# Retention values of two heads projected in one pass of 512 moving columns, after all kv blocks

## The chip, the core and the metric

One NeuronCore of a Trainium2 chip runs the whole program; seven others are idle. The metric is the device time of one execution in microseconds (us), as the median of several. TensorE (PE) multiplies, ScalarE (ACT) and VectorE (DVE) move results out of its accumulators (PSUM, eight banks of 128 x 512 float32) and do the arithmetic between, GpSimd (POOL) does a few small steps, and SyncE (SP) issues the loads. Each engine works through a queue of its own; semaphores hold an instruction until what it reads is there.

## What is computed

One decoder block on 512 tokens of 1024 features, in float32. Cut to the part that the change touches:

```python
h = rmsnorm(x, pre_mix_norm)
proj = h @ w_in                     # (512, 5888)
q_r, k_r, v_r, g_r, q_s, k_s, v_s, gate_r, gate_s = split(proj)
ret = retention_chunkwise(q_r, k_r, v_r)     # 4 heads: dk 128, dv 256, chunks of 128 tokens
ret = silu(g_r) * ret
swa = swa_gqa_sinks(q_s, k_s, v_s, sinks)    # 8 query heads, 2 key/value heads of 64
merged = sigmoid(gate_r) * (ret @ w_ret_out) + sigmoid(gate_s) * (swa @ w_swa_out)
x = x + rmsnorm(merged @ w_out, post_mix_norm)
x = x + rmsnorm(square(relu(rmsnorm(x, pre_mlp_norm) @ w_up)) @ w_down, post_mlp_norm)
```

The values v_r of the four retention heads are columns 1024 to 2047 of the projection, 256 a head; the keys and values of the windowed attention (kv) are 256 columns more.

## The kernel before

Every float32 operand is split into a high and a low part that TensorE takes in one pass each (`split`, L104: ACT casts the high part, DVE subtracts for the low one), and a product is three matmuls (`mm3`, L147): high by high, high by low, low by high. Operands of weights are cast by `parts` (L112), into tiles `whi` and `wlo` of which four of each exist; loads land in two tiles `raw` of 1 MB.

The tokens are four blocks of 128. `norm_tokens` (L274) squares and sums a block on ACT, takes the power on POOL, scales on DVE (two instructions), transposes eight times on TensorE and splits the result into `hT`, features by tokens. A block can be projected in two ways. `project_block` (L312, tile `pblk`) has weights standing still and all 512 tokens moving: 24 matmuls of 512 columns give 128 output columns, features by tokens. `project_token_block` (L299, tile `ptok`) has one block of tokens standing still and 256 columns of weights moving: 24 matmuls of 256 columns give 128 tokens of 256 outputs. The values and the kv columns are wanted with tokens in rows, so they go the second way.

At the start (L338 to L350) the kv blocks and the value blocks of head 0 alternate: norm of token block 0, its kv block, norm of block 1, value block 0, kv block 1, norm of block 2, value block 1, and so on. Value block 3 follows later (L582), behind the first query projection and the transposes of the windowed keys. Then the loop over four heads (L583): scores of the windowed attention, projection of the retention queries, the output transposes of the head before, projection of the retention keys, transposes of the probabilities and keys, values of the *next* head (`project_v`, L305, in rounds 0 to 2), scores, windowed values, states, gates and, between the two gate blocks, the next head's windowed queries, and the retention outputs. The fourth round projects no values.

The order of the instructions in each engine's queue is settled when the program is built, from the order of the code, what each instruction depends on and which buffers are free, and is fixed from then on. The stretch around the change reads:

```python
    norm_tokens(0)
    w_kv = moving_parts(raw_kv)
    kv_block(0)
    norm_tokens(1)
    w_v0 = moving_parts(raw_v0)
    v0_block(0)
    kv_block(1)
```

Of the kernel before, what the change touches and what calls it, by code (L numbers as in the profile page):

```python
# [16 lines left out]
P = 128  # L17
D_MODEL = 1024
SEQ = 512
NT = SEQ // P  # L20
# [26 lines left out]
def decay_table():  # L47
    """[j, h, i]: gamma_h ** -(j + 1) / sqrt(dk) where i >= j, else 0; within a chunk."""
    pos = np.arange(P)
    t = np.where(  # L50
        pos[None, :] >= pos[:, None],
        np.exp(-log_gammas()[:, None, None] * (pos[:, None] + 1)), 0.0,
    )
    return np.ascontiguousarray((t * RET_DK**-0.5).transpose(1, 0, 2).astype(np.float32))


def chunk_table():
    """[j, 0, h]: gamma_h ** (127 - j) / sqrt(dk); [i, 1, h]: EPS * gamma_h ** (-2 (i + 1))."""
    pos, lg = np.arange(P)[:, None], log_gammas()[None, :]
    t = np.stack([np.exp(lg * (P - 1 - pos)) * RET_DK**-0.5, EPS * np.exp(-2 * lg * (pos + 1))], 1)  # L60
    return np.ascontiguousarray(t.astype(np.float32))


def distance_table():
    """[i, j]: distance of query i to key j of the two blocks, or MASKED / slope-free mask."""
    dist = (np.arange(P)[:, None] + P) - np.arange(2 * P)[None, :]
    return np.where((dist >= 0) & (dist < P), -dist, MASKED).astype(np.float32)
# [7 lines left out]
def block_kernel(ctx, tc, x, pre_mix, w_in, w_ret, w_swa, w_out, sinks, post_mix,  # L75
# [20 lines left out]
    def rstd_of(sumsq, n, scale):  # L96
        """(sumsq * scale + eps) ** -0.5, [P, n]."""
        ms = small.tile([P, 4], F32, name="ms")
        r = small.tile([P, 4], F32, name="rstd")
        nc.vector.tensor_scalar(ms[:, :n], sumsq, scale, EPS, op0=ALU.mult, op1=ALU.add)  # L100
        nc.gpsimd.tensor_tensor(r[:, :n], ms[:, :n], mhalf[:, :n], op=ALU.pow)
        return r

    def split(hi, lo, src):  # L104
        """src = hi + lo exactly, each with a significand that one pass carries."""
        nc.scalar.copy(hi, src)  # L106
        nc.vector.tensor_tensor(lo, src, f(hi), op=ALU.subtract)  # L107
# [10 lines left out]
    def load_feature_pair(w, c0):  # L118
        """Columns c0..c0+256 of w as two stationary blocks [k, kk, 128]."""
        nk = w.shape[0] // P  # L120
        raw = raw_tile([P, nk, 256])
        nc.sync.dma_start(raw, w[:, c0 : c0 + 256].rearrange("(k p) c -> p k c", p=P))
        return [parts(raw[:, :, b * P : (b + 1) * P], [P, nk, P]) for b in range(2)]

    def load_feature_blocks(w, cols):
        """Columns c..c+128 of w, for each c, as stationary blocks [k, kk, 128]."""
        nk = w.shape[0] // P
        raw = raw_tile([P, 2, nk, P])
        for b, c0 in enumerate(cols):
            nc.sync.dma_start(raw[:, b], w[:, c0 : c0 + P].rearrange("(k p) c -> p k c", p=P))  # L130
        return [parts(raw[:, b], [P, nk, P]) for b in range(len(cols))]

    def load_moving(w, r0, nr, c0, width):
        """Rows r0.. of w, columns c0..c0+width, as moving blocks, two tiles."""
        raw = raw_tile([P, nr, width])
        nc.sync.dma_start(
            raw, w[r0 * P : (r0 + nr) * P, c0 : c0 + width].rearrange("(k p) c -> p k c", p=P)
        )
        return moving_parts(raw)
# [12 lines left out]

    # ---- one level of Strassen-Winograd for a pair of output feature blocks:
    # rows of the product are the two blocks, its columns the two token halves,
    # the contraction is halved too.
    def wino_pool(stack, side="left"):
        return stack.enter_context(tc.tile_pool(name="wx", bufs=1, side=side))

    def wino_tokens(wx, b11, b12, b21, b22, f, dst):
        """b: (hi, lo) quadrants; f: their float32 copies, overwritten; dst: (hi, lo) of sums."""  # L160
        f11, f12, f21, f22 = f
        nc.vector.tensor_tensor(f11, f11, f12, op=ALU.subtract)
        split(dst[0][:, 0], dst[1][:, 0], f11)
        nc.vector.tensor_tensor(f12, f22, f12, op=ALU.subtract)
        split(dst[0][:, 2], dst[1][:, 2], f12)
        nc.vector.tensor_tensor(f22, f22, f11, op=ALU.add)
        split(dst[0][:, 1], dst[1][:, 1], f22)
        nc.vector.tensor_tensor(f21, f22, f21, op=ALU.subtract)
        split(dst[0][:, 3], dst[1][:, 3], f21)
        sums = [tuple(d[:, i] for d in dst) for i in range(4)]  # L170
        return {"11": b11, "21": b21, "22": b22, "t1": sums[0], "t2": sums[1],
                "t3": sums[2], "t4": sums[3]}

    def wino_weights(wx, w, c0):
        """Columns c0..c0+256 of w: the seven left operands, (hi, lo) of [k, 4, 128]."""
        raw = raw_tile([P, KD, 256])
# [22 lines left out]
    def wino_pair(wx, a, b, out):  # L199
        """out [P, 4, 256]: the two halves of block one, then those of block two, negated."""  # L200
        p16 = bank([P, 2, 256], "wino")
# [28 lines left out]

    # ---- pools by phase
    hctx = ExitStack()
# [3 lines left out]
    def transpose_in(dst, src_of, half):  # L236
        """token-major [P, 1024] blocks (of two token blocks) -> feature-major hi, lo."""
        for kp in range(KD // 2):
# [11 lines left out]

    # ---- pre-norm of x, kv and first v projection by token block
    bctx = ExitStack()
    kvpool = bctx.enter_context(tc.tile_pool(name="kvpool", bufs=1))
    kv = kvpool.tile([P, NT, 256], F32, name="kv")
    v_next = [kvpool.tile([P, NT, RET_DV], F32R, name=f"v{i}", bufs=2) for i in range(2)]
    xctx = ExitStack()
# [17 lines left out]
    def norm_tokens(t):  # L274
        """Token block t of the normed input, transposed, as hi and lo."""
        ss = small.tile([P, 2], F32, name="ss")
# [27 lines left out]

    def project_v(h):  # L305
        w = load_moving(w_in, 0, KD, C_VR + h * RET_DV, RET_DV)
        v = [kvpool.tile([P, NT, RET_DV], F32R, name=f"v{i}", bufs=2) for i in range(2)]
        for t in range(NT):
            split(v[0][:, t, :], v[1][:, t, :], project_token_block(w, t))
        return v  # L310

# [12 lines left out]
    load_x(1)  # L324
    raw_v0 = load_raw(C_VR)
    load_x(2)
# [5 lines left out]
    def kv_block(t):  # L332
        nc.scalar.copy(kv[:, t, :], project_token_block(w_kv, t))

    def v0_block(t):
        split(v_next[0][:, t, :], v_next[1][:, t, :], project_token_block(w_v0, t))

    norm_tokens(0)  # L338
    w_kv = moving_parts(raw_kv)
    kv_block(0)  # L340
    norm_tokens(1)
    w_v0 = moving_parts(raw_v0)
    v0_block(0)
    kv_block(1)
    norm_tokens(2)
    v0_block(1)
    kv_block(2)
    norm_tokens(3)
    v0_block(2)
    kv_block(3)  # L350
    xctx.close()
# [16 lines left out]

    # ---- sliding-window attention, one pair of heads (2b, 2b + 1)
    def swa_queries(w):  # L370
        """Both heads' scaled queries, each with hi and lo stacked along the contraction."""
        ps = project_block(w)
# [99 lines left out]

    # ---- retention, one head, by chunks of 128 tokens; token i of a chunk is carried
    # divided by gamma ** (i + 1), which the group norm takes out again
    def ret_keys(kT, h):
        """Token-major keys of the first three chunks, decayed to the chunk's end."""
        ps = bank([P, NT - 1, P], "ret_k")
# [23 lines left out]
    def ret_states(kd, v, h):  # L501
        """State before chunks 1, 2 and 3."""
        decayed = float(np.exp(log_gammas()[h] * P))
# [69 lines left out]
    for g in range(SWA_KV):  # L573
# [7 lines left out]
        split(ksT[0][:, g, :], ksT[1][:, g, :], ps)  # L581
    v0_block(3)  # L582
    for h in range(RET_HEADS):  # L583
# [13 lines left out]
        kd = ret_keys(kT, h)  # L597
        v = v_next
        if h + 1 < RET_HEADS:
            v_next = project_v(h + 1)  # L600
        pt = ret_scores(qT, kT, h)
# [14 lines left out]

    # ---- swa output projection
    def swa_out(fb, ws):
# [28 lines left out]

    # ---- gates
    gctx = ExitStack()
# [32 lines left out]
    def ret_proj(bp):  # L682
        """Output projection of the retention, gated, plus the gated swa's, in sig."""
        wr = load_feature_pair(w_ret, bp * 256)
# [18 lines left out]

    # ---- output projections of both mixers, merge
    mpool = ctx.enter_context(tc.tile_pool(name="mpool", bufs=16))
# [31 lines left out]

    # ---- output projection, residual, pre-norm of the MLP
    gpool = ctx.enter_context(tc.tile_pool(name="gpool", bufs=1, side="right"))
# [49 lines left out]

    # ---- MLP  # L790
    GB = 8
# [93 lines left out]
    def finish(t, n):  # L885
        """Post-norm and residual of token block t, once acc's column half n is whole."""
        c = slice(n * 512, (n + 1) * 512)
# [92 lines left out]
```

## Time and profile before

| | |
|---|---|
| median of 3 runs | 774.61 us (774.47 to 774.65) |
| span of the profiled execution, first to last instruction | 772.8 us |
| TensorE (PE) busy | 761.1 us |
| VectorE (DVE) busy | 510.3 us |
| ScalarE (ACT) busy | 367.6 us |
| mean granted TensorE clock | 0.997 of full speed |
| `ptok` matmuls, 256 columns | 480, of them 384 for values, 96 for kv |
| `pblk` matmuls, 512 columns | 480 |

The profiler records one execution. A line of the timeline gives the start in us, the duration, the engine, the line of the kernel, the operation, `output tile<-input tiles`, the shapes and how many instructions are merged in it; in brackets the idle time ahead of it and what ended it. Matmuls overlap in the record, so what one costs is the distance from start to start, not its duration. Lines of a helper such as L107 or L149 serve many callers; the tile names tell them apart.

### The profile page before, as it was taken

The page shows a single profiled execution, that of the slowest core. Times are in us where ns is not written, and L with a number is a line of the kernel's source. Part 1 is how long each engine was busy: PE and PEld are TensorE (multiplying, and loading weights), DVE is VectorE, ACT ScalarE, POOL GpSimd, SP SyncE. Part 2 cuts the span into 40 slices and gives each one's busy share as a digit, 9 for nine tenths or more (in the row PEclk, how much of TensorE's full clock was granted, in tenths as well). Part 3 has the DMA queues.
Part 4 walks back from the last instruction along what each step waited for, and adds up shares of the span by engine and source line. Part 5 has one row for each costly group of instructions (what it writes and reads, how often), then busy time and mean ns, then how long its engine had stood idle before and what let it go on. Part 6 is the DMA issues. An engine that isn't in the chain of part 4 may idle for free.

```text
span 772.8 us, 11585 instructions
## 1 busy us (share of the span) xinstructions
PE 761.1 (98%) x4772; PEld 686.5 (89%) x4772; DVE 510.3 (66%) x841; ACT 367.6 (48%) x619; POOL 19.2 (2%) x30
## 2 busy tenths in 40 slices
PE   8999999999999999999999999999999999999996
PEld 6989889898888999999888999999999999999885
DVE  5474474655878888775954887665667675766364
ACT  6364454364644535333634785545544444444321
POOL 1100000000001000000011000000000000000000
PEclk9999999999999999999999999999999999999998
DMA  9151222312012333243571133333323333222402
GB/s 295 28 163 53 90 58 75 109 29 81 28 58 80 120 125 115 68 146 109 185 251 54 56 109 109 110 109 110 93 81 100 109 110 109 87 81 106 137 1 109
DMA packets 68038, 78.21 MB, mean 101 GB/s; under 512 B 1809, under 2 KB 55185, under 8 KB 67986
## 3 DMA queue, kind: packets, MB, share of 16 engines
q1 hardware_dynamic: 67986, 77.48, 31.3%
q8 instruction: 37, 0.61, 0.3%
q14 instruction: 15, 0.12, 0.1%
HBM read 75.38 MB, written 2.10 MB: 100 GB/s over the span
## 4 chain that ended last, share of the span: by engine, by line
PE 93%; DVE 3%; ACT 1%; issue 1%; DMA 1%; POOL 0%; SPq 0%; DVEq 0%; POOLq 0%; ACTq 0%
PE wino L149 9%; PE wino L151 9%; PE wino L150 9%; PE down L149 7%; PE down L150 7%; PE down L151 7%; PE pblk L151 5%; PE pblk L150 5%; PE pblk L149 5%; PE ptok L151 2%; PE ptok L150 2%; PE ptok L149 2%; PE yr L149 2%; PE ps L149 2%; PE ps L151 2%; PE yr L151 2%
## 5 line engine op out<-in xcount | busy, mean ns | idle before, releaser
L106 ACT CAST whi<-raw 128x1024 fp32r<-128x1024 f32 x103 | 107.9, 1051 | 127.1 <-PE down L151 57.7
L107 DVE TENSOR_TENSOR wlo<-raw,whi 128x1024 fp32r<-128x1024 f32 x103 | 125.4, 1221 | 63.0 <-ACT whi L106 53.6
L149 PE MATMUL down<-whi,u 128*128 128x512 f32 x256 | 99.8, 390 | 0.0
L150 PE MATMUL down<-wlo,u 128*128 128x512 f32 x256 | 99.7, 390 | 0.0
L151 PE MATMUL down<-whi,u 128*128 128x512 f32 x256 | 99.6, 389 | 0.0
L151 PE MATMUL pblk<-hT,wlo 128*128 128x512 f32 x160 | 62.4, 390 | 0.5 <-DVE wlo L107 0.5
L149 PE MATMUL pblk<-hT,whi 128*128 128x512 f32 x160 | 62.6, 391 | 0.0
L150 PE MATMUL pblk<-hT,whi 128*128 128x512 f32 x160 | 62.3, 390 | 0.0
L151 PEld LDWEIGHTS down<-whi,u 128*128 128x128 f32 x256 | 48.1, 188 | 10.0
L149 PEld LDWEIGHTS down<-whi,u 128*128 128x128 f32 x256 | 48.1, 188 | 9.6
L150 PEld LDWEIGHTS down<-wlo,u 128*128 128x128 f32 x256 | 48.1, 188 | 9.6
L149 PE MATMUL ptok<-whi,hT 128*128 128x256 f32 x160 | 46.1, 288 | 0.3 <-ACT hT L106 0.3
L106 ACT CAST whi<-s 128x1024 fp32r<-128x1024 f32 x21 | 22.0, 1049 | 51.1 <-PE wino L150 26.3
L151 PE MATMUL ptok<-whi,hT 128*128 128x256 f32 x160 | 45.4, 283 | 0.8 <-DVE hT L107 0.8
L150 PE MATMUL ptok<-wlo,hT 128*128 128x256 f32 x160 | 45.4, 284 | 0.0
L107 DVE TENSOR_TENSOR u<-rl,u 128x512 fp32r<-128x512 f32 (+1 forms) x38 | 22.1, 605 | 24.5 <-ACT u L106 24.5
L221 DVE TENSOR_TENSOR q<-wino,q 128x512 f32<-128x512 f32 x21 | 14.5, 691 | 34.4 <-PE wino L151 34.4
L151 PEld LDWEIGHTS pblk<-hT,wlo 128*128 128x128 f32 x160 | 30.0, 188 | 7.2 <-DVE wlo L107 0.9
L149 PEld LDWEIGHTS pblk<-hT,whi 128*128 128x128 f32 x160 | 30.1, 188 | 5.8
L150 PEld LDWEIGHTS pblk<-hT,whi 128*128 128x128 f32 x160 | 30.0, 188 | 5.8
L151 PEld LDWEIGHTS ptok<-whi,hT 128*128 128x128 f32 x160 | 30.6, 192 | 1.1 <-DVE hT L107 1.1
L149 PEld LDWEIGHTS ptok<-whi,hT 128*128 128x128 f32 x160 | 30.8, 192 | 0.7 <-ACT hT L106 0.7
(261 smaller groups left out, 2118.6 us busy)
## 6 DMA issues: line engine op xcount, KB each, us to landing
raw<-in_w_in SPq DMA_DIRECT2D x17, 1024.0 KB, 5.2
raw<-in_w_up SPq DMA_DIRECT2D x17, 1024.0 KB, 5.6
raw<-in_w_down SPq DMA_DIRECT2D x16, 1024.0 KB, 4.9
raw<-in_w_in SPq DMA_DIRECT2D x12, 512.0 KB, 4.4
raw<-in_w_ret_out SPq DMA_DIRECT2D x4, 1024.0 KB, 5.2
raw<-in_w_out SPq DMA_DIRECT2D x4, 1024.0 KB, 5.0
xt<-in_x SPq DMA_DIRECT2D x4, 512.0 KB, 8.1
raw<-in_w_swa_out SPq DMA_DIRECT2D x4, 512.0 KB, 3.5
```

The source lines that it names most:

```text
L106: nc.scalar.copy(hi, src)
L107: nc.vector.tensor_tensor(lo, src, f(hi), op=ALU.subtract)
L149: nc.tensor.matmul(ps, ah, bh, start=first, stop=False)
L150: nc.tensor.matmul(ps, ah, bl, start=False, stop=False)
L151: nc.tensor.matmul(ps, al, bh, start=False, stop=last)
L221: nc.vector.tensor_tensor(q[:, 1:3], p57, q[:, 0:1].to_broadcast([P, 2, 256]), op=ALU.add)
```

## The change

The values of two heads become one projection of 512 moving columns. The weights come in two loads of four row blocks by 512 columns, each cast into two pairs of tiles; a block of 128 tokens takes 24 matmuls of 512 columns into one whole bank, and one split writes both heads' values. The value tiles have the same size in all (two of two heads' width in place of four of one head's). At the start the kv blocks come right behind the norms, with no value block between; the four value blocks of heads 0 and 1 follow all of them, and none is left for behind the key transposes. Those of heads 2 and 3 stand in the third round of the head loop; the first, second and fourth round have none. The load of value weights that stood between the first and second later token loads is gone; the new loads are issued behind all token loads.

```diff
-    v_next = [kvpool.tile([P, NT, RET_DV], F32R, name=f"v{i}", bufs=2) for i in range(2)]
+    def v_tiles():
+        return [kvpool.tile([P, NT, 2 * RET_DV], F32R, name=f"v{i}", bufs=1) for i in range(2)]
+
+    v2 = v_tiles()
...
-    def project_v(h):
-        w = load_moving(w_in, 0, KD, C_VR + h * RET_DV, RET_DV)
-        v = [kvpool.tile([P, NT, RET_DV], F32R, name=f"v{i}", bufs=2) for i in range(2)]
-        for t in range(NT):
-            split(v[0][:, t, :], v[1][:, t, :], project_token_block(w, t))
-        return v
+    def load_v(h):
+        return load_moving(w_in, 0, 4, C_VR + h * RET_DV, 2 * RET_DV) + load_moving(
+            w_in, 4, 4, C_VR + h * RET_DV, 2 * RET_DV
+        )
+
+    def v_block(v, w, t):
+        ps = bank([P, 2 * RET_DV], "pv")
+        for k in range(KD):
+            mm3(ps, hcol(k, t), w[k], k == 0, k == KD - 1)
+        split(v[0][:, t, :], v[1][:, t, :], ps)
...
-    raw_v0 = load_raw(C_VR)
...
-    norm_tokens(1)
-    w_v0 = moving_parts(raw_v0)
-    v0_block(0)
-    kv_block(1)
-    norm_tokens(2)
-    v0_block(1)
-    kv_block(2)
-    norm_tokens(3)
-    v0_block(2)
-    kv_block(3)
+    for t in range(1, NT):
+        norm_tokens(t)
+        kv_block(t)
+    w_v = load_v(0)
+    for t in range(NT):
+        v_block(v2, w_v, t)
...
-    v0_block(3)
...
-        v = v_next
-        if h + 1 < RET_HEADS:
-            v_next = project_v(h + 1)
+        if h == 2:
+            v2, w_v = v_tiles(), load_v(h)
+            for t in range(NT):
+                v_block(v2, w_v, t)
+        v = [a[:, :, (h % 2) * RET_DV : (h % 2 + 1) * RET_DV] for a in v2]
```

## Rows read from the trace of the kernel before

**Rows 1.** Head of the page: busy us, share of the span, instructions of each engine.
```profile
PE 761.1 (98%) x4772; PEld 686.5 (89%) x4772; DVE 510.3 (66%) x841; ACT 367.6 (48%) x619; POOL 19.2 (2%) x30
```
**Rows 2.** TensorE's waits, first 320 us: total us, times, longest us.
```profile
PE ptok L151 <- DVE hT L107: 0.8, 1, 0.8
...
PE pblk L151 <- DVE wlo L107: 0.5, 1, 0.5
...
PE swa_s L405 <- DVE qs L378: 0.2, 1, 0.2
```
**Rows 3.** Timeline, TensorE: first of 96 value matmuls in round 0, and what follows.
```profile
59.66 0.36 PE L149 MATMUL ptok<-whi,hT 128*128 128x256 f32 x1
...
71.26 1.05 PE L492 MATMUL ret_s<-qT,kT 128*128 128x128 f32 x8
```
**Rows 4.** Timeline, TensorE: two runs of 48 matmuls of 512 columns, first and next.
```profile
46.89 0.40 PE L149 MATMUL pblk<-hT,whi 128*128 128x512 f32 x1
...
57.81 0.60 PE L446 MATMUL psd<-ident,s 128*128 128x128 f32 x4
...
470.33 0.40 PE L149 MATMUL down<-whi,u 128*128 128x512 f32 x1
...
481.24 0.28 PE L149 MATMUL wino<-h2c,whi 128*128 128x256 f32 x1
```
**Rows 5.** Timeline, TensorE and DVE: transposes of token blocks 1 and 3, low parts.
```profile
14.34 1.04 PE L289 MATMUL tin<-ident,hn 128*128 128x128 f32 x8
15.13 0.36 PE L149 MATMUL ptok<-whi,hT 128*128 128x256 f32 x1
...
27.85 1.03 PE L289 MATMUL tin<-ident,hn 128*128 128x128 f32 x8
...
29.11 1.29 DVE L107 TENSOR_TENSOR hT<-tin,hT 128x512 fp32r<-128x512 f32 x2 [3.11 <-ACT hT L106]
```
**Rows 6.** Windows: busy time of each engine, granted clock, DMA share, GB/s.
```profile
9.70:14.30 4.60, 3.44 (x25) 3.19 (x25) 3.93 (x8) 4.31 (x7) 0.56 (x1) 1.00 1.06 376
```
**Rows 7.** Timeline, DVE: norm of token block 1, value weights' casts, its low parts.
```profile
12.89 1.41 DVE L283 SCALAR_TENSOR_TENSOR hn<-xt,rstd,g_pre 128x512 f32<-128x512 f32 x2 [0.67 <-POOL rstd L101]
14.21 2.35 DVE L107 TENSOR_TENSOR wlo<-raw,whi 128x1024 fp32r<-128x1024 f32 x2
16.48 1.28 DVE L107 TENSOR_TENSOR hT<-tin,hT 128x512 fp32r<-128x512 f32 x2
```
**Rows 8.** Timeline, TensorE, ACT, DVE: value block 3, first window scores, queries, keys.
```profile
41.53 0.36 PE L149 MATMUL ptok<-whi,hT 128*128 128x256 f32 x1
...
44.49 1.11 PE L405 MATMUL swa_s<-ksT,qs 128*128 128x256 f32 x8
...
41.66 0.59 ACT L377 ACTIVATE qs<-pblk 64x512 fp32r<-64x512 f32 x1
...
43.05 0.69 DVE L378 SCALAR_TENSOR_TENSOR qs<-pblk,qs 64x512 fp32r<-64x512 f32 x1
43.76 1.29 DVE L107 TENSOR_TENSOR ksT<-ps,ksT 128x512 fp32r<-128x512 f32 x2
```
**Rows 9.** Timeline, round 2: first value matmul on TensorE, weight casts behind the keys.
```profile
161.39 0.36 PE L149 MATMUL ptok<-whi,hT 128*128 128x256 f32 x1
...
162.47 1.09 ACT L106 CAST whi<-raw 128x1024 fp32r<-128x1024 f32 x1
...
163.59 1.23 DVE L107 TENSOR_TENSOR wlo<-raw,whi 128x1024 fp32r<-128x1024 f32 x1 [0.32 <-ACT whi L106]
```
**Rows 10.** Timeline, TensorE, 416 us: transposes between matmuls of one output block.
```profile
416.70 1.91 PE L829 MATMUL tin<-ident,zg 128*128 128x128 f32 x16
418.36 0.47 PE L150 MATMUL ps<-wo,mhi 128*128 128x512 f32 x1
```
**Rows 11.** Timeline, TensorE, round 3: scores and states, no values between.
```profile
212.33 1.06 PE L492 MATMUL ret_s<-qT,kT 128*128 128x128 f32 x8
...
216.13 0.39 PE L149 MATMUL ret_st<-v,kd 128*128 128x256 f32 x1
```

More of the change, by code (lines that the diff above doesn't have):

```diff
@@ L333, in kv_block @@
         nc.scalar.copy(kv[:, t, :], project_token_block(w_kv, t))
-    def v0_block(t):
-        split(v_next[0][:, t, :], v_next[1][:, t, :], project_token_block(w_v0, t))
     norm_tokens(0)
```

## Prediction, made before the changed kernel was built or run

> **What bounds the kernel now.** I read the head of the page first, then TensorE's waits, then TensorE's timeline from the start to the end of the fourth head. The head of the page shows a TensorE that is busy for 761.1 us, 98% of the span [rows 1]; that share alone says little, but the list of its waits does: behind the first kv block's start TensorE waited for 0.8, 0.5 and 0.2 us in the stretch that the change touches, and for nothing longer [rows 2]. So the time is the spacing of the matmuls, one behind the other, and a change is worth what it takes from that spacing, less the waits that it opens. The profiled span is 772.8 us, the median 774.61 us; the 1.8 us between them I carry over unchanged.
>
> **The change, part by part.**
>
> *Width of the v projections.* One head's values are 96 matmuls of 256 columns. In the first head round they run from 59.66 to 71.26 us, where the next work starts: 11.60 us, 120.8 ns each [rows 3]. Four heads make 384 of them, 46.4 us. The change issues 192 matmuls of 512 columns in their place. Two places show that form: 48 of them with weights standing still, 46.89 to 57.81 us, and 48 with weights moving, as they will be here, 470.33 to 481.24 us: 10.92 and 10.91 us, 227.4 ns each [rows 4]. 192 x 0.2274 = 43.7 us. The saving is 46.4 - 43.7 = **2.7 us**, 14.2 ns for each pair of narrow matmuls, all of it on TensorE and so on the path.
>
> A rule speaks for less. The Trainium skill, "TensorE: Matmul & The Clock Gate", section "Back-to-back issue gap", gives a warm spacing of the columns over 2.4 GHz plus 2.5 ns; as an estimate from that page a wide matmul in place of two narrow ones would save 2.5 ns, 0.5 us in all, and the time would be near 774.1. The trace does not agree with it: the rows above have 14.2 ns, and the measured number goes into the sum.
>
> *The wait for the query weights.* Now TensorE waits 0.5 us for the low part of the first query block [rows 2], because the buffer for its cast comes free only in the last kv block, one short block ahead. After the change that buffer is the first of the v weights', last read by the sixth of 24 matmuls of the last v block, 18 x 0.227 = 4.1 us ahead of its use; a cast is 1.09 on ACT and 1.23 on DVE [rows 9]. The wait goes: **-0.5**.
>
> *The kv blocks without v blocks between them.* This is what the change gives up. A token block is normed (two DVE instructions, 1.41 us [rows 7]), transposed, cast to a high part by ACT and a low part by DVE, and then read by a kv block, whose third matmul wants the low part. Now a v block of the token before stands between, so the chain is hidden. Its length is seen at the last token: transposes from 27.85 us, low part's first half done at 29.11 + 0.64 = 29.75 [rows 5]: 1.90 us. TensorE fills 0.79 of it with the eight transposes themselves (14.34 to 15.13 [rows 5]) and 0.24 with two matmuls; **0.87 us per token** is bare if nothing else is put there, 2.6 for three tokens. That is the upper bound; the lower is nothing, if other work steps in.
> Whether it does depends on the order in each engine's queue, which is fixed before the run. The trace shows that this order isn't that of the code: DVE took the v weights' casts at 14.21 ahead of the first token's low parts at 16.48, which the code issues earlier [rows 7], and TensorE took sixteen transposes at 416.70 in the middle of a block, whose other matmuls follow at 418.36 [rows 10]. So work that is ready goes ahead of work that isn't. What can be ready: the transposes of the next token, and then the v block of token 0. Token 1: its norm ends at 12.89 + 1.41 = 14.30 as now [rows 7]; DVE no longer has the two v casts (2.35 us from 14.21) behind it, so it norms token 2 until 15.71 and writes the first low part until 16.36. TensorE has 1.23 us from 15.13 till then; two matmuls and the next token's transposes take 1.03 of it: I charge **0.25**. Token 2: its low part is done about 18.3, while the kv block of token 1 runs until about 19.05: **0**. Token 3: its transposes come behind a kv block again, and only the first v block can fill the 0.87. Its weights' casts need 2.4 us of DVE after the last norm, some 22 us, about when they are wanted, so I charge half, **0.45** (0 to 0.87). TensorE's clock over such a gap: with 1.16 us idle of 4.6 the granted clock is 1.00, the level of 2.4 GHz [rows 6], so I put nothing on the clock.
>
> *The last block of head 0's values* now stands behind the key transposes and covers the queries' and keys' casts: it runs from 41.53 to 44.49, and the scores behind it still waited 0.2 us [rows 2, 8]. After the change nothing in the code stands there. Bare, the chain would be: the projection's last matmul is done some 0.6 us before 41.53 (the eight key transposes between take 0.8 us, and it ends 0.2 us into them), then ACT's query copy 0.59, DVE's 0.69, one key low part 0.65 (half of 1.29 [rows 8]): scores at about 42.9, 1.35 us after 41.53. Bounds 0 to 1.35. The next projection (48 matmuls, 10.92 us [rows 4]) needs only its weights, cast during the projection before, so it can step in; I charge 0, and take off the 0.2: **-0.2**.
>
> *Loads and buffers.* The v weights come as two loads of 1 MB in place of four, each cast in two tiles as before; four cast tiles are held in place of two. The first load replaces one that stood ahead of two token loads, so tokens 2 and 3 have 1 MB less ahead of them; the second load waits on SP for the kv weights' casts, and behind it wait the small tables and the first query weights, wanted 20 us later. No charge. The tiles for its casts come free inside the last kv block; casts of 1.09 and 1.23 us then stand against 12 wide matmuls (2.7 us) that need only the first load. No charge.
>
> *Rounds 0 and 1 lose a projection between the key transposes and the scores.* Round 3 has none there now, and TensorE runs through: scores at 212.33, states at 216.13 with no idle time [rows 11]. **0.** *Round 2* holds all four wide blocks. The last of the four cast tiles is that of the keys' weights; its casts fall where those behind the keys' block fall now, ACT 162.47, DVE 163.59 to 164.82, and the first v block, begun as now at 161.39 [rows 9], wants it 18 wide matmuls later, at 165.5. **0**, with 0.7 us of slack.
>
> **Sum:** -2.7 - 0.5 + 0.25 + 0.45 - 0.2 = **-2.7 us**: 774.6 - 2.7 = **771.9**; its own bounds are 771.2 (no bare chain at all) and 773.0.
>
> **The rivals.** *Code order holds at the start of TensorE's queue*: nothing steps in. With the transposes still moved ahead, 0.25 + 0.87 + 1.35 us are bare against -3.2: 773.9. With nothing moved, 2.6 + 1.35: 775.4. For it: TensorE stood 0.5 us before the query weights with a v block ready behind them [rows 2, 8], and nothing stepped in. Against it: the transposes of [rows 10].
> *DVE becomes the bound of the start, and the kernel is slower.* From 10 to 20 us DVE is near full already, 3.93 of 4.60 us between 9.70 and 14.30 [rows 6]. If the v weights' casts take the place on DVE that they have now (14.21 to 16.56, ahead of the low parts and of the next norm [rows 7]), but without a v block on TensorE to cover it, the low part of token 1 comes at 17.1 instead of 15.4 (1.7 us bare), token 2's norm at 19.9 and its chain behind (1.15), token 3's 0.9, and the scores' 1.35: 5.1 - 3.2 = +1.9, 776.5. It decides from about 4.7 us of bare time. For it: that order was chosen in this very trace; against it: the code now issues those casts after all norms, so whatever is ready of a norm goes first.
> The Trainium skill, on the same page, section "HAM oscillation — how this bites in real kernels", warns that gaps between bursts of matmuls bring the half clock back, which would make such a start slower still; the gap above kept its 1.00.
> *The wide form saves nothing here*, two narrow spacings for one wide: then -0.7 + 0.7, 774.6. The rows with moving weights speak against it [rows 4].
>
> **How the numbers follow.** Forecast 0.58; code order 0.27 (773.9 to 775.4); DVE-bound start 0.11 (776.5); no saving 0.04. About 0.2%, 1.55 us, can be told from no change: faster is below 773.06, slower above 776.16. Faster 0.58, same 0.30 (code order and no saving, less a little), slower 0.12. The range takes in the forecast's own 771.2, a little under it, and code order up to 775.4.
>
> **What would show it.** Right: 96 wide matmuls of a v pair in 21.8 us, twice; no idle time in front of round 2's third and fourth weight tile; TensorE's waits before 30 us under 1.5 us beyond the first kv block's; matmuls of a v block or transposes standing between a token's transposes and its kv block. Wrong: kv blocks each preceded by a wait of 0.9 us for a low part, a wait of over 1 us before the first scores, v casts ahead of norms on DVE, or a spacing of the wide form above 0.23 us.

## The result, and the profile after

The changed kernel is slower: 779.08 us (778.57 to 779.16, 4 runs) against 774.63 us (774.47 to 775.98, 4 runs) of the kernel before on the same chip, a ratio of 1.0047 [1.0032, 1.0061] (the ratios here are the record's estimates with their 95% intervals; the two medians alone would give 1.0057). The forecast was 771.9, and its range ended at 775.4. The profiled execution spans 777.3 us where that of before has 772.8: +4.5 us to be found. One thing is needed to read the ratios below: on both chips of the experiments the kernel before itself lies on two levels, 774.5 to 774.8 and 775.7 to 776.2 us with a few runs above, so its median there is 775.84 and 775.98.

Head of the page of the changed kernel, to be held against [rows 1]:

```profile
span 777.3 us, 11189 instructions
...
PE 761.8 (98%) x4580; PEld 679.5 (87%) x4580; DVE 511.1 (66%) x833; ACT 367.4 (47%) x611; POOL 20.0 (3%) x30
```

And TensorE's waits over the whole span (total us, times, longest us), to be held against [rows 2]:

```profile
PE swa_s L407 <- DVE qs L380: 3.2, 1, 3.2
...
PE ptok L151 <- DVE hT L107: 1.1, 1, 1.1
```

TensorE has 192 matmuls fewer, yet its busy time is 0.7 us longer. The busy share hides this: a slowly clocked matmul is busy too. The list of waits shows one new entry that stands out, 3.2 us in front of the first window scores, where before had 0.2. The wait for the low part of the query weights (`pblk <- DVE wlo`, 0.5) is gone, as forecast.

To find the rest I cut TensorE's timelines of before and after at the same events and took the differences. The v projections are counted apart, by start to start: 24 wide matmuls for a token block, 227.4 ns each, against 48 narrow of 120.8 [rows 3, 4].

| stretch of TensorE's timeline | before, us | after, us | change |
|---|---|---|---|
| end of kv block 0 (start of the next transposes) | 14.34 | 15.90 | +1.56 |
| from there to the first query projection, less v matmuls | 11.44 | 12.35 | +0.91 |
| the first query projection | 6.26 | 5.45 | -0.81 |
| key transposes to the next projection, less v matmuls | 3.25 | 8.02 | +4.77 |
| the next two projections | 10.92 | 11.10 | +0.18 |
| rest of the four rounds, less v matmuls | 138.08 | 138.37 | +0.29 |
| all behind them | 542.11 | 542.45 | +0.34 |
| v matmuls of all heads | 46.39 | 43.66 | -2.73 |
| sum | | | +4.51 |

Two stretches carry the loss. The larger one, TensorE's timeline of the changed kernel from the key transposes on (start, duration, engine, line, operation; idle time and what ended it in brackets):

```profile
55.53 1.03 PE L580 MATMUL ps<-ident,kk 128*128 128x128 f32 x8
59.72 0.47 PE L407 MATMUL swa_s<-ksT,qs 128*128 128x256 f32 x2 [3.16 <-DVE qs L380]
60.35 3.40 PE L407 MATMUL swa_s<-ksT,qs 128*128 128x256 f32 x14 [0.16 <-DVE ksT L107]
63.55 0.58 PE L149 MATMUL pblk<-hT,whi 128*128 128x512 f32 x1
```

TensorE waits 3.16 us, and then the 14 scores take 3.20 us, 229 ns each, where gaplessly fed ones below take about 119. The windows of the same kernel (us, PE busy, PEld, DVE, ACT, POOL, granted clock, DMA share, GB/s) say why:

```profile
60.00:62.00 2.00, 1.84 (x9) 1.54 (x8) 1.94 (x6) 0.20 (x1) 0.00 (x0) 0.64 0.91 258
62.00:64.00 2.00, 2.00 (x10) 1.91 (x10) 2.00 (x13) 0.39 (x2) 0.00 (x0) 0.51 0.02 4
64.00:66.00 2.00, 2.00 (x10) 1.67 (x9) 1.86 (x12) 2.00 (x12) 0.00 (x0) 1.00 0.00 0
```

Behind the idle stretch the granted clock is 0.64, then 0.51, the 1.2 GHz level, and then 1.00 again. The prediction cited the Trainium skill, "TensorE: Matmul & The Clock Gate", section "HAM oscillation — how this bites in real kernels", on gaps that bring the half clock back; in this place the trace agrees with it, 0.51 behind 3.16 us without a matmul.

What TensorE waits for is the queries' low parts on DVE (L380). The timelines of ACT, then DVE, then of SP's load issues, all of the changed kernel:

```profile
55.41 2.00 ACT L106 CAST whi<-raw 128x1024 fp32r<-128x1024 f32 x2 [4.54 <-DMA raw<-in_w_in]
57.31 0.59 ACT L379 ACTIVATE qs<-pblk 64x512 fp32r<-64x512 f32 x1
...
47.33 3.91 DVE L107 TENSOR_TENSOR wlo<-raw,whi 128x1024 fp32r<-128x1024 f32 x3 [1.18 <-ACT whi L106]
...
56.50 2.36 DVE L107 TENSOR_TENSOR wlo<-raw,whi 128x1024 fp32r<-128x1024 f32 x2 [4.66 <-ACT whi L106]
58.89 0.68 DVE L380 SCALAR_TENSOR_TENSOR qs<-pblk,qs 64x512 fp32r<-64x512 f32 x1
...
49.95 0.37 SPq L122 DMA_DIRECT2D raw<-in_w_in  x1
```

The queries are in the accumulator at about 55.7, but ACT copies them only at 57.31 and DVE subtracts at 58.89, because both have two casts of other weights ahead of them in their queues. These are the gate weights of round 0 (loaded in L122), wanted much later in the round. ACT idles 4.54 us in front of its first cast, waiting for the load; SP issued that load at 49.95, and in the kernel before at 43.04 (its timeline of SP):

```profile
43.04 0.38 SPq L122 DMA_DIRECT2D raw<-in_w_in  x1
```

It is issued late because its `raw` tile comes free late. The casts of the first three weight blocks of round 0 (three in 47.33 to 51.24 on DVE, 1.3 us each) have to wait for cast tiles that the last v block reads; the second of them is done at about 49.9, and SP issues at 49.95.

The load's delay is not the whole of it. Seen from the key transposes it is issued earlier than before, 5.6 us ahead of their start (49.95 against 55.53) and not 2.3 us behind it (43.04 against 40.74). What is new is the place of its casts: in the kernel before ACT takes the first of them at 53.23, told by the order of the loads, long behind the first query copy at 41.66 [rows 8]. One cast of other weights, the retention keys', stood in front of the first query's low part on DVE there too, at 41.79. The timelines of ACT, then DVE, of the kernel before:

```profile
53.23 1.05 ACT L106 CAST whi<-raw 128x1024 fp32r<-128x1024 f32 x1
...
41.79 1.23 DVE L107 TENSOR_TENSOR wlo<-raw,whi 128x1024 fp32r<-128x1024 f32 x1 [4.54 <-PE ps L578]
```

The other stretch is the first kv block. TensorE's timeline of the changed kernel, two neighbouring matmuls out of it and the next transposes:

```profile
13.13 0.41 PE L151 MATMUL ptok<-whi,hT 128*128 128x256 f32 x1
13.34 0.41 PE L149 MATMUL ptok<-whi,hT 128*128 128x256 f32 x1
...
15.90 1.17 PE L294 MATMUL tin<-ident,hn 128*128 128x128 f32 x8
```

The windows there:

```profile
12.00:14.00 2.00, 2.00 (x14) 2.00 (x14) 1.33 (x4) 1.97 (x4) 0.56 (x1) 0.69 1.04 384
14.00:16.00 2.00, 2.00 (x11) 2.00 (x11) 1.40 (x5) 0.08 (x1) 1.07 (x2) 0.50 1.04 384
```

From 12.7 to 15.9 the matmuls stand 0.21 us apart and not 0.12, at a granted clock of 0.69 and 0.50, behind a wait of 1.06 us. In before's profile the same place kept 1.00 [rows 6]. It costs about 1.4 us; the other 0.2 of the +1.56 is a later start.

### The profile page after: what moved, and what is told of

Its sections match the earlier page's. It is cut to its first block, busy times and chain, and to the rows that moved or that the text cites. A ratio compares the mean times of both kernels' runs of the same rounds, so it can differ in the third digit from the quotient of the medians.

```text
span 777.3 us, 11189 instructions
## 1 busy us (share of the span) xinstructions
PE 761.8 (98%) x4580; PEld 679.5 (87%) x4580; DVE 511.1 (66%) x833; ACT 367.4 (47%) x611; POOL 20.0 (3%) x30
## 4 chain that ended last, share of the span: by engine, by line
PE 91%; DVE 4%; ACT 2%; DMA 1%; issue 1%; POOL 0%; SPq 0%; DVEq 0%; POOLq 0%; ACTq 0%
PE wino L151 9%; PE wino L149 9%; PE wino L150 9%; PE down L149 7%; PE down L150 7%; PE down L151 7%; PE pblk L149 4%; PE pblk L150 4%; PE pblk L151 4%; PE yr L149 2%; PE ps L149 2%; PE yr L150 2%; PE ps L151 2%; PE yr L151 2%; PE ps L150 2%; PE pv L149 2%
## 5 line engine op out<-in xcount | busy, mean ns | idle before, releaser
L151 PE MATMUL wino<-h2c,wlo 128*128 128x256 f32 x104 | 29.4, 283 | 0.0
L149 PE MATMUL wino<-h2s,p 128*128 128x256 f32 x104 | 29.4, 283 | 0.0
L150 PE MATMUL wino<-h2s,p 128*128 128x256 f32 x104 | 29.4, 283 | 0.0
L151 PE MATMUL wino<-h2s,p 128*128 128x256 f32 x104 | 29.4, 283 | 0.0
L149 PE MATMUL wino<-h2s,whi 128*128 128x256 f32 x104 | 29.4, 283 | 0.0
```

Source lines behind the costliest of these rows:

```text
L149: nc.tensor.matmul(ps, ah, bh, start=first, stop=False)
L150: nc.tensor.matmul(ps, ah, bl, start=False, stop=False)
L151: nc.tensor.matmul(ps, al, bh, start=False, stop=last)
```

## The experiments

Theory A: the loss is the wait at the scores with the slow clock behind it, and the wait comes from the order in ACT's and DVE's queues, where the gate weights' casts stand ahead of the queries'. Theory B: it is the slow clock at the start. Theory C: the wide form with moving weights saves less in this place than its rows promised. Theory D: the gap at the scores is what the move itself costs, whatever the order of the casts. The added matmuls of four kernels below write a bank that nobody reads.

**The first gap filled.** Eight matmuls in the wait ahead of the first kv block, nothing else.

```diff
     w_kv = moving_parts(raw_kv)
+    fill = bank([P, 256], "fill")
+    for _ in range(8):
+        nc.tensor.matmul(fill, hcol(0, 0)[0], w_kv[0][0], start=True, stop=True)
     kv_block(0)
```

> Eight matmuls whose result nobody reads stand between the first token's transposes and its kv block, so that TensorE isn't idle while the low parts are on their way; nothing else differs from the changed kernel. In the changed kernel the granted clock fell to 0.50 from about 12.7 to 15.9 us, behind an idle stretch of 1.06 us, which cost 1.4 us. If that idle stretch brings the clock down, the granted clock stays 1.00 there and the time is 779.1 - 1.4 = 777.7. If the fall has nothing to do with it, 779.1 and the same fall.

Measured: 778.09 us (777.15 to 779.49, 7 runs), 1.0033 [1.0022, 1.0045]. The windows of this kernel:

```profile
12.00:14.00 2.00, 2.00 (x19) 2.00 (x18) 1.33 (x4) 1.90 (x4) 0.56 (x1) 1.00 1.05 388
14.00:16.00 2.00, 1.76 (x15) 1.52 (x14) 1.40 (x5) 1.34 (x4) 1.07 (x2) 1.00 1.03 382
```

The clock stays at 1.00 and the first kv block takes 3.25 us (11.14 to 14.39). The wait of 3.17 us at the scores and the clock of 0.65 and 0.50 behind it remain. So B is worth 1.0 us between the medians, and most of the loss is elsewhere. The first kv block ends 1.5 us earlier (14.39 against 15.90), but the token blocks behind it take 0.4 us longer, so the first query projection starts 1.06 us earlier (49.02 against 50.08).

**The wait at the scores filled.** Fourteen matmuls of 512 columns behind the key transposes keep TensorE busy; they remove no wait of another engine.

```diff
         split(ksT[0][:, g, :], ksT[1][:, g, :], ps)
+    fill2 = bank([P, SEQ], "fill2")
+    for _ in range(14):
+        nc.tensor.matmul(fill2, hcol(0, 0)[0], hrow(0)[0], start=True, stop=True)
     for h in range(RET_HEADS):
```

> Fourteen matmuls of 512 columns, read by nobody, stand behind the key transposes, where TensorE waits 3.2 us for the queries; the wait for the queries itself is left as it is. If the slow scores behind that wait (16 matmuls in 3.8 us, granted clock about 0.5) are the clock's answer to the idle time, the scores still start at about 59.7 but run in 2.1 us: 779.1 - 1.7 = 777.4. If something else makes them slow (DVE reading the banks, say), 779.1.

Measured: 777.31 us (776.48 to 778.17, 10 runs), 1.0026 [1.0017, 1.0035]. TensorE's timeline:

```profile
55.93 3.43 PE L586 MATMUL fill<-hT 128*128 128x512 f32 x14
59.37 0.36 PE L407 MATMUL swa_s<-ksT,qs 128*128 128x256 f32 x1
...
62.38 0.40 PE L149 MATMUL pblk<-hT,whi 128*128 128x512 f32 x1
```

And a window of it:

```profile
60.00:62.00 2.00, 1.77 (x12) 1.57 (x13) 1.94 (x7) 0.00 (x0) 0.00 (x0) 1.00 0.84 246
```

The first score starts about as late as without the filling, but the clock is 1.00, and the next projection starts 3.0 us behind the first score (59.37 to 62.38) and not 3.8 (59.72 to 63.55); the two projections behind take 10.91 us and not 11.10. So the slow clock behind the idle stretch costs 1.0 us in this place, net of the waits among the scores, which are 0.5 us here and 0.16 where the scores run slowly. The medians differ by 1.8 us; the other 0.8 lies outside this place and is not shown to be the clock's. The wait itself is still paid.

**The gate weights' casts behind the queries'.** The casts of round 0's gate weights are put behind the first window queries' on ACT and DVE; nothing else changes. Their load stays where it was: SP issues it at 50.01, against 49.95 in the changed kernel.

```diff
-            nc.scalar.mul(q2[rows[g]], ps[rows[g]], SWA_DH**-0.5)
-            nc.vector.scalar_tensor_tensor(
+            qs_last[0] = nc.scalar.mul(q2[rows[g]], ps[rows[g]], SWA_DH**-0.5)
+            qs_last[1] = nc.vector.scalar_tensor_tensor(
...
-        g = load_feature_pair(w_in, C_GR + h * RET_DV)
+        if h == 0:
+            with tc.issue_after(qs_last[0].ins), tc.issue_after(qs_last[1].ins):
+                g = load_feature_pair(w_in, C_GR + h * RET_DV)
+        else:
+            g = load_feature_pair(w_in, C_GR + h * RET_DV)
```

> The two casts of round 0's gate weights are queued behind the casts of the first window queries on ACT and DVE; in the changed kernel they stand ahead of them and wait for a load that lands at 55.4 us. If those casts hold up the queries (ACT 1.6 us, DVE 2.4), the first scores start at about 57.7 in place of 59.7: 2.0 us less, and 1.7 more if the shorter idle stretch leaves the clock alone: 775.4 to 777.1. If the queries' own chain is what takes so long, 779.1.

Measured: 775.36 us (774.4 to 776.28, 10 runs), 0.9996 [0.9987, 1.0005]. TensorE's timeline, then ACT's:

```profile
57.24 0.47 PE L409 MATMUL swa_s<-ksT,qs 128*128 128x256 f32 x2 [0.62 <-DVE qs L382]
57.88 0.98 PE L409 MATMUL swa_s<-ksT,qs 128*128 128x256 f32 x6 [0.16 <-DVE ksT L107]
59.20 1.22 PE L409 MATMUL swa_s<-ksT,qs 128*128 128x256 f32 x8 [0.34 <-DVE qs L382]
60.26 0.40 PE L149 MATMUL pblk<-hT,whi 128*128 128x512 f32 x1
...
55.79 0.59 ACT L381 ACTIVATE qs<-pblk 64x512 fp32r<-64x512 f32 x1 [4.86 <-PE pblk L151]
...
57.98 2.00 ACT L106 CAST whi<-raw 128x1024 fp32r<-128x1024 f32 x2
```

ACT copies the queries 1.5 us earlier and the gate casts follow at 57.98. The waits at the scores are 0.62 + 0.16 + 0.34 us, no slow clock follows, and 3.7 of the lost microseconds are back. In the profile 3.35 of them lie in this place: from the key transposes to the next projection it takes 4.67 us (55.59 to 60.26) in place of 8.02. That is A. What remains of the move, the bare chain of queries and keys, is 1.1 us of waits, and 1.4 us on the stretch against the 3.25 of the kernel before: about the prediction's upper bound of 1.35 for it, so D holds only for this remainder.

**Narrow matmuls in the changed order.** Everything as changed, but each v block in two runs of 24 matmuls of 256 columns.

```diff
-        for k in range(KD):
-            mm3(ps, hcol(k, t), w[k], k == 0, k == KD - 1)
+        for j in range(2):
+            c = slice(j * RET_DV, (j + 1) * RET_DV)
+            for k in range(KD):
+                mm3(ps[:, c], hcol(k, t), tuple(a[:, c] for a in w[k]), k == 0, k == KD - 1)
```

> The changed kernel with each value block as two runs of 24 matmuls of 256 columns in place of 24 of 512: same loads, casts and places, only the width undone. In this kernel the gate casts happen to stand behind the queries' casts too, as in the kernel that queues them late, so it is that kernel it is to be compared with. If the width is worth 2.7 us as forecast, it is 2.7 us slower than that one: 778.1 to 779.8. If the width is worth nothing, it is level with it: 775.4 to 777.1.

Measured: 778.91 us (778.57 to 779.31, 4 runs), 1.0044 [1.0029, 1.0059], the changed kernel's own time. That looks as if the width were worth nothing, but its trace has no wait of 3.2 us: the scores wait 1.0 and 0.2 us in all, because in this build the gate weights' casts stand behind the queries' on ACT, as in the kernel just above: ACT's first query copy is held up by nothing but TensorE, and the gate casts start at 60.03, behind the second copy.

```profile
57.85 0.59 ACT L381 ACTIVATE qs<-pblk 64x512 fp32r<-64x512 f32 x1 [4.26 <-PE pblk L151]
```

The fair partner is that one, and against it the narrow form is 3.55 us slower. TensorE's timeline of the third round's v projections, narrow in this kernel (first v matmul, and what follows the last):

```profile
153.87 0.36 PE L149 MATMUL pv<-whi,hT 128*128 128x256 f32 x1
...
176.98 1.05 PE L496 MATMUL ret_s<-qT,kT 128*128 128x128 f32 x8
```

And wide, in the changed kernel:

```profile
155.24 0.48 PE L149 MATMUL pv<-whi,hT 128*128 128x512 f32 x1
...
177.12 1.05 PE L494 MATMUL ret_s<-qT,kT 128*128 128x128 f32 x8
```

23.11 us against 21.88, 1.2 us for a pair, 2.5 for both. The two profiled executions are 3.1 us apart (776.8 and 773.7), which is these 2.5 and a wait of its own of 0.6 us (`pv <- DVE wlo`); the other 0.5 us between the medians is not located. Theory C falls: the wide form saves what its rows said.

**The changed kernel once more**, beside the three below.

> The changed kernel unaltered, beside the experiments' runs of the kernel before. Both theories: near 779.1, ratio 1.0047. It also says how its runs spread: if the early fall of the clock comes in some executions only, two levels 1.4 us apart as in the runs of the kernel before; if the change always brings it, one level.

Measured: 779.12 us (778.0 to 780.47, 6 runs), 1.0049 [1.0037, 1.0062]. By its ratio the loss is the same on another chip, and the wait at the scores is there again with 3.1 us. The runs do not lie on two levels 1.4 us apart: four are at 779.0 to 779.3, one at 778.0, one at 780.5. The profiled one is that at 778.0, and it too has the slow spacing at the start, 0.21 us from 12.05 to 14.83, behind a wait of only 0.8 us.

**The last part of the values kept as a cover.** The v projections of heads 0 and 1 are gathered in four banks, quarter by quarter of the contraction; three quarters come at the start, and the last, 24 wide matmuls, behind the key transposes, where before had a v block.

```diff
-    for t in range(NT):
-        v_block(v2, w_v, t)
+    pv = [bank([P, 2 * RET_DV], "pv") for _ in range(NT)]
+
+    def v_part(kq):
+        for t in range(NT):
+            for k in (2 * kq, 2 * kq + 1):
+                mm3(pv[t], hcol(k, t), w_v[k], k == 0, k == KD - 1)
+
+    for kq in range(3):
+        v_part(kq)
     xctx.close()
...
+    for kq in range(3, 4):
+        v_part(kq)
+    for t in range(NT):
+        split(v2[0][:, t, :], v2[1][:, t, :], pv[t])
     for h in range(RET_HEADS):
```

> The first pair's values are gathered over the contraction in quarters, all four token blocks in each, in four banks; the last quarter (24 matmuls of 512 columns, 5.4 us) stands behind the key transposes, where the kernel before had its last value block. Same matmuls, loads and casts. If the change lost its time by leaving nothing to cover the queries' and keys' casts, the wait of 3.3 us before the scores and their slow clock (1.7) go: 779.1 - 5.0 = 774.1. If the gate casts ahead of the queries' hold the scores up in any case, a wait of 1 to 3 us stays: 775 to 778.

Measured: 773.06 us (772.31 to 773.98, 6 runs), 0.9967 [0.9954, 0.9979], faster than before. TensorE's timeline:

```profile
50.81 0.48 PE L149 MATMUL pv<-whi,hT 128*128 128x512 f32 x1
...
56.35 2.07 PE L414 MATMUL swa_s<-ksT,qs 128*128 128x256 f32 x16
58.26 0.40 PE L149 MATMUL pblk<-hT,whi 128*128 128x512 f32 x1
```

No wait ahead of the scores; all 16 take 1.91 us, 119 ns each. The cover is worth more than the late casts alone, since the chain of queries and keys is hidden with it: 6.1 us below the changed kernel. From the key transposes to the next projection, less the v matmuls, it takes 2.78 us (50.02 to 58.26, less 24 x 0.2274), against 4.67 with the late casts and 3.25 before. Two more things differ in this build, as ACT's timeline shows:

```profile
49.99 1.05 ACT L106 CAST whi<-raw 128x1024 fp32r<-128x1024 f32 x1 [4.16 <-PE pblk L150]
...
57.03 1.05 ACT L106 CAST whi<-raw 128x1024 fp32r<-128x1024 f32 x1
```

Only the first gate cast still stands ahead of the queries' copy (50.94), the second behind, and their load is issued at 41.72, so that no cast waits for it. What the cover does against two casts that wait is therefore not shown; that it hides the chain is.

**The three together.** This cover, the filled first gap, and the gate weights' casts behind the queries'.

> The cover of k_outer, the gate casts queued behind the first window queries' casts, and the eight matmuls that fill the first idle stretch, together. By the theory (cover, casts, clock) all that the change lost is back and the width's 2.7 us and the 0.5 us of the query weights stay: 771.9 to 773.3, ratio to the kernel before 0.997 to 0.999. If the loss lies elsewhere, above 775.

Measured: 772.3 us (772.11 to 772.41, 5 runs), 0.9957 [0.9945, 0.9969]. It beats both kernels, and by 2.2 us even the lower level of before. Head of its page:

```profile
span 770.6 us, 11202 instructions
...
PE 759.5 (99%) x4588; PEld 677.3 (88%) x4588; DVE 510.0 (66%) x833; ACT 366.5 (48%) x611; POOL 20.0 (3%) x30
```

And the two longest of TensorE's waits:

```profile
PE g_pre L275 <- DMA g_row<-in_pre_mix_norm: 2.4, 1, 2.4
PE wino L149 <- ACT whi L106: 0.5, 1, 0.5
```

The first stands ahead of all matmuls, before any data is there; the second belongs to a later stage that the change doesn't touch. Behind them no wait of TensorE is longer than 0.4 us, and it has 2.3 us less busy time than the changed kernel.

**The kernel before with its first gap filled.** The same eight matmuls ahead of before's first kv block, to see whether the two levels of before are the clock at the start.

> The kernel before with the eight matmuls that fill its first idle stretch of 0.84 us; nothing else. Its own runs lie on two levels, near 774.6 and near 776.0. If the upper level is the clock falling behind that idle stretch in some executions, every run of this one lies on the lower level, 774.2 to 774.9. If the two levels come from elsewhere, both stay.

Measured: 774.7 us (774.47 to 776.12, 11 runs), 0.9991 [0.9982, 0.9999]. 3 of 11 runs are at 775.88 or above; of the kernel before beside it, 13 of 18 are at 775.7 or above. So the upper level became rarer, but it did not go away. Not all that brings it is the gap that I filled, or filling it does not always hold the clock; none of these runs tells which.

## Why the prediction was wrong, step by step

*Width: right.* 2.7 us forecast, 2.73 in the table above, and the third round's pair took 21.88 us against the 21.8 named as the sign. The Trainium skill, "TensorE: Matmul & The Clock Gate", section "Back-to-back issue gap", gives its 2.5 ns for the gap of a single, isolated matmul; the estimate of 0.5 us saved that was made from it stays at odds with the trace: 14.2 ns a pair.

*The wait for the query weights: right.* Gone; the whole projection is 0.81 us shorter against the 0.5 charged.

*The kv blocks without v blocks: right in kind, its size partly luck.* 0.7 us charged, 0.91 found. But the slow first kv block hid some of it: in the kernel with the first gap filled, at the full clock that the charge assumed, the same stretch is 0.44 us longer, 1.35. Work stepped in as argued. TensorE, changed kernel: six of the next token's transposes behind two matmuls of a kv block, and before the last token's third matmul three of the first v block.

```profile
17.31 0.39 PE L149 MATMUL ptok<-whi,hT 128*128 128x256 f32 x1 [0.24 <-ACT hT L106]
17.54 0.28 PE L150 MATMUL ptok<-wlo,hT 128*128 128x256 f32 x1
17.66 0.82 PE L294 MATMUL tin<-ident,hn 128*128 128x128 f32 x6
...
25.65 0.40 PE L149 MATMUL pv<-whi,hT 128*128 128x512 f32 x1
...
26.34 0.28 PE L151 MATMUL ptok<-whi,hT 128*128 128x256 f32 x1
```

*"The last block of head 0's values": wrong, and this is the step that failed.* It was charged nothing, less 0.2, with 1.35 as the upper bound; it cost 4.8. Three parts of it failed. First, the next projection was to step in, since its weights were cast in time. They were (the three casts on DVE end at 51.24), but TensorE's queue keeps the scores ahead of it; that the order at the start isn't the code's does not carry over to this place. Second, the upper bound took the chain of queries and keys as if ACT and DVE were free for it. Its waits are 1.1 us when they are, as the kernel with the late casts shows, and 3.3 when two casts stand in front, which the bound did not look at. The rows to ask were there: in [rows 8] ACT's copy ends at 42.25 and DVE's subtraction starts only at 43.05, behind the cast of other weights at 41.79. Third, the clock behind the idle stretch, 1.0 us in place by the kernel that filled it. Of the 4.8 us, 3.35 go with the two casts in front, the clock included, and 1.4 are the bare chain. The sum's upper bound was too low besides: with the upper ends of its own terms (0.25, 0.87, 1.35, against 3.2 saved) it is 773.9 and not 773.0.

*"Loads and buffers ... No charge": wrong in the second half.* The v loads themselves cost nothing. But four cast tiles held to the last v block push the first query weights' casts from about 33 us to 46, so their `raw` tile comes free late, so the gate weights' load is issued only at 49.95, and it is the first of the two casts that ACT then idles for. The step asked whether those casts are in time for their own projection, which they are, and not what is loaded into the tile that they free. That an earlier load alone would have removed the wait is argued from these times; no run moves the load alone. That the order of the casts makes the wait is shown: with the load at 50.01 and the casts behind the queries', it is gone.

*"I put nothing on the clock": wrong by 1.4 us at the start, of which 1.0 reaches the end, and by about 1.0 at the scores.* At the start the one profile of before showed 1.00 [rows 6], and I took it for a property of the gap. The change did not lengthen that gap by much (1.06 us against 0.8 [rows 2]). But it is not the gap's length: in its second profile the changed kernel waits 0.8 us, as before does, and has the slow spacing. All six profiles of the changed order without the eight matmuls ahead of the first kv block have it; the one of before and the three with these matmuls do not. One profile of before is too few to say that the change makes it more frequent; the upper level of before lies about 1.4 us above the lower, the same size as the loss in that stretch.

*Rounds 0 to 2: right to 0.3 us.* The rivals: DVE did not become the bound of the start, the v weights' casts came behind the norms. Code order held at the scores alone, and its bare 1.35 us would have ended at 773.9 with the transposes moved; neither rival had the casts in the queue. The wide form saved what it promised.

## What to carry to other kernels

A block of work that is moved away may have been the cover of a short chain on the other engines; price that chain with everything that stands in those engines' queues in between, casts of later weights above all, and follow each tile that is freed later to the load that it holds back. An idle stretch of TensorE can cost more than its length, through the slow clock behind it: here 3.2 and 1.0 us. Where a projection is the only cover at hand, it need not move as a whole: a quarter of its contraction, left behind, was enough here, with the gate casts no longer held up, to keep the gain of the wider form.

## What was not expected of the hardware

The clock can fall to its 1.2 GHz level behind a wait of 0.8 to 1.1 us at the start, which costs 1.4 us there. It did so in both profiles of the changed kernel and in four more of its order, and not in that of before, with the same wait of 0.8; where eight matmuls filled the wait it did not, in three profiles of three. The record of the granted clock does not always show it. In the kernel with the late casts the window reads 1.00, while the matmuls inside it stand 0.21 to 0.22 us apart, the spacing that went with 0.50 above; 256 columns at 1.2 GHz are 0.213 us. The window from 12 to 14 us reads 1.00 with that spacing in two more profiles, the changed kernel's second and that of the filled wait at the scores. That it is the clock there too is concluded from the spacing. TensorE's timeline of the kernel with the late casts:

```profile
12.81 0.41 PE L150 MATMUL ptok<-wlo,hT 128*128 128x256 f32 x1
13.03 0.41 PE L151 MATMUL ptok<-whi,hT 128*128 128x256 f32 x1
```

And its window:

```profile
12.60:13.60 1.00, 1.00 (x6) 1.00 (x6) 0.75 (x2) 0.97 (x3) 0.22 (x1) 1.00 1.05 385
```

So the spacing from start to start is worth reading beside the column. What else lifts a run of the kernel before to its upper level stays open.
